# Hybrid attention and convolution step: 38 of 64 input-projection tiles computed in pairs by seven block products, conv taps spread into the attention

## The chip, the cores and the metric

One core of a Trainium2 chip runs the whole kernel. PE multiplies matrices (PEld is its loading of stationary operands), DVE and ACT work element by element, POOL too but cannot read PSUM, and SP issues nearly all DMAs. The metric is the device time of one execution in microseconds, as the median of several runs. Profiled executions come with a trace, from which all times by engine and line are read.

## The reference

The layer is one inference step of a streaming encoder, for 1024 new frames of one stream and 32 frames of a running one; the kernel puts them side by side as 1056 tokens. All data is float32.

```python
q = rmsnorm(cols(OFF_Q, ATTN_WIDTH).reshape(B, T, N_HEADS, HEAD_DIM), q_g) * (HEAD_DIM ** -0.5)
k = rmsnorm(cols(OFF_K, ATTN_WIDTH).reshape(B, T, N_HEADS, HEAD_DIM), k_g)
v = cols(OFF_V, ATTN_WIDTH).reshape(B, T, N_HEADS, HEAD_DIM)
logf = jax.nn.log_sigmoid((cols(OFF_F, N_HEADS) + b_f).astype(jnp.float32))
ga = cols(OFF_GA, ATTN_WIDTH)
u = cols(OFF_UA, CONV_WIDTH) * jax.nn.sigmoid(cols(OFF_UB, CONV_WIDTH))
gb, ma, mb = cols(OFF_GB, CONV_WIDTH), cols(OFF_MA, D_MODEL), cols(OFF_MB, D_MODEL)
...
ya = (o_attn.reshape(B, T, ATTN_WIDTH) * jax.nn.silu(ga)) @ w_pa
yb = (jax.nn.silu(layernorm(conv, ln_g, ln_b)) * jax.nn.silu(gb)) @ w_pb
m = jax.nn.sigmoid(ma) * ya + jax.nn.sigmoid(mb) * yb
return x + m @ w_out
```

`cols(a, w)` is `rmsnorm(x) @ w_in[:, a:a + w]`. `o_attn` is causal softmax attention of 16 heads of 64 with a bias from the running sum of `logf`; `conv` is a causal depthwise convolution of `u` over 31 taps. The widths are 1024, so eight of the nine projections are 1024 x 1024 (`logf` has 16 columns), and three more such products follow the branches.

## The kernel before

**Plain projections.** `xh` and `xl` hold the normalised input as a high part (float32r) and a remainder, with 8 blocks of 128 channels on the partitions and 1056 tokens in a row. A *tile* is 128 output channels of one projection: `steps` (L144) takes its weights, split by ACT into `wh` (L91) and by POOL into the remainder `wl` (L94), and multiplies over three pieces of 352 tokens and 8 channel blocks. Each of these 24 steps is three matmuls (`mms`, L102): xh by wh, xh by wl, xl by wh. A tile is so 72 matmuls of 352 columns. The nine projections but `v` and `logf` make 64 tiles: ub, ua, k, q, ga, gb, ma, mb, 8 each. `v` and `logf` are computed the other way round, with 260 weight columns moving (L582).

**Order.** PE, DVE and ACT follow program order up to the attention, and PE all through. `beat` (L118) is called once a step: it runs what `later(n, fn)` put off by n beats, and adds `pace["rate"]` to a credit from which *conv taps* are paid. A tap (`conv_taps`, L248) is one DVE instruction on 128 x 1086 elements (L258); 30 of them and one ACT instruction make the convolution of one channel tile f, and then come its LayerNorm sums (`sums`: L228, L235, L236, L241).

**Stages.** The input is normalised and turned while the first ub and ua tiles run (to 44 us). Then come u tiles 1 and 2 among the four parts of v (to 193 us), u tile 3, and for each f the k and q tiles, with u tiles 4 to 7 between them. `qk` (L678) squares each piece on ACT, sums squares by head with two small matmuls (L697, L698), takes the root on ACT (L700, L701), scales on DVE (L704) and stores high and low parts for the attention (L714, L715). Then u tile 7 and the 8 ga tiles (to about 591 us). In these stages taps of channel tiles 0 to 6 run on DVE beside the matmuls.

**Attention** (591 to 1095 us). Per head there are 8 blocks of 128 queries, and 4 blocks of the running stream among them. A block's scores (L905, L906) go to PSUM three blocks ahead of its use; DVE adds the mask and takes the maximum (L908, L910), ACT the exponentials (L913), DVE the reciprocal (L915), POOL the scaling (L916); PE turns the result (L926) and multiplies by V (L940). Between blocks PE does 4 steps of a plain tile (`fill`); 22 tiles (gb, ma, 6 of mb) are done so. The 31 taps of channel tile 7 and its sums run here, one tap for each 8 steps, and then the LayerNorm statistics (`layernorm`, one step a block).

**End.** Two mb tiles, then the three products of the branches (`outproj`), 8 tiles each.

Of the kernel before, what the change touches and what calls it, by code (L numbers as in the profile page):

```python
# [16 lines left out]
T = 1024  # L17
TS = 32
# [12 lines left out]
NFILL = 22  # L31
R_U, R_V, R_QK, R_G, R_A = 0.25, 0.17, 0.19, 0.27, 0.12
# [16 lines left out]
def build(tc, xT, xt, wv, wf, ckT, cv, clT, stT, vec, cst, yT, kT, vO, lfO, cpT, csT):  # L49
# [19 lines left out]
    s_m = dram.tile([128, TT], F32, name="s_m")  # L69

    cp = pool("cp")
    wp = pool("wp", 2)
# [3 lines left out]
    rawp = [wp]  # L76
# [11 lines left out]
    def split_w(raw, offset=2000):  # L88
        with tc.high_priority(offset=offset):
            wh = wp.tile([128, KT, 128], F32R, name="wh", tag="wh")  # L90
            nc.scalar.copy(wh, raw)  # L91
            wl = wp.tile([128, KT, 128], F32R, name="wl", tag="wl")
            for k0, k1 in WSP:
                nc.gpsimd.tensor_sub(wl[:, k0:k1, :], raw[:, k0:k1, :], f32(wh[:, k0:k1, :]))  # L94
        return wh, wl
# [40 lines left out]
    def fetch():  # L136

        if plan:
            key = plan.pop(0)
            if not plan:  # L140
                rawp[:] = [wp]
            split[key] = split_v(key[1]) if key[0] == "v" else split_w(load_raw(key))
# [27 lines left out]
    sg = pool("sg")  # L170

    def t352(name, bufs):
        return sg.tile([128, CH], F32, name=name, tag=name, bufs=bufs)

    pq = pool("pq", 1, space=PS)
    pps = ExitStack()
    pjA = pool("pjA", 4, stack=pps, space=PS)
# [15 lines left out]
    cvp = pool("cvp", 2, stack=pcv)  # L193
    us = {}
    taps = []
    cvt = [cvp]
# [9 lines left out]
    def shift_of(y):  # L206

        shift = cvp.tile([128, TT], F32, name="shift", bufs=1)
        ones = cvp.tile([128, 128], F32, name="ones", bufs=1)
# [8 lines left out]
        nc.sync.dma_start(s_m, shift)  # L218
# [28 lines left out]

    def conv_taps(f):  # L248
        u = us.pop(f)

        def tap(i):
            w = vec_t[:, V_WDW + f * KC + i:V_WDW + f * KC + i + 1]
            if i == 0:
                y = sides["y", f] = cvt[0].tile([128, CW], F32, name="y", tag="y")
# [3 lines left out]
            t = nc.vector.scalar_tensor_tensor(y, u[:, i:i + CW], w, y, op0=ALU.mult, op1=ALU.add)  # L258
            if f == 7:
                tc.keep_in_program_order(t)  # L260
            if i == KC - 1:
                kept(f, y)

        items = [lambda i=i: tap(i) for i in range(KC)]
        if f == 7:
            taps.extend(pend + items)
# [11 lines left out]
    def u_tile(f):  # L278
        if f > 2:
            pump(len(taps) - 66)  # L280
        u = us[f] = cvt[0].tile([128, UW], F32, name="u", tag="u", bufs=3 if f < 7 else 1)
# [4 lines left out]
    def u_done(f):  # L286
        u = us[f]
# [71 lines left out]
    os_t = cp.tile([128, 8, TS], F32, name="os_t")  # L359
# [116 lines left out]
    plan.extend([("ub", 1), ("ua", 1), ("v", 0), ("v", 1), ("ub", 2), ("ua", 2), ("v", 2), ("v", 3), ("ub", 3), ("ua", 3)])  # L476
    for f in range(8):
        if f in (2, 4, 6):
            plan.extend([("ub", 3 + f // 2), ("ua", 3 + f // 2)])
        plan.extend([("k", f), ("q", f)])  # L480
    plan.extend([("ub", 7), ("ua", 7)] + [("ga", f) for f in range(8)] + [("gb", 0)])
# [23 lines left out]
    prw = ExitStack()  # L505
    rxs = [pool(f"rx{i}", 1, stack=prw) for i in range(2)]
    rawp.extend(rxs)
# [3 lines left out]
    p2 = ExitStack()  # L511
    u7p = pool("u7p", 1, stack=p2, side="right")
    pv = ExitStack()
    zp = pool("zp", 1, stack=pv, side="right")
    z = zp.tile([128, 9, H], F32, name="z")
# [45 lines left out]
    for c in range(4):  # L561
        if c == 2:
            pace["rate"] = R_U
            u_proj(2, pj)
            while ("y", 0) not in sides or len(taps) > 62:
# [28 lines left out]
    fp = pool("fp", 1, stack=pv, side="right")  # L594
# [3 lines left out]
    def small(name):  # L598
        return fp.tile([128, NZ], F32, name=name, tag=name)

    lf = fp.tile([128, 9, H], F32, name="lf")
    lfs = lf, lf.rearrange("p a b -> p (a b)")

    def log_sigmoid():
        lf, lff = lfs
        az, ee, s2, ac = small("az"), small("ee"), small("s2"), small("ac")
# [19 lines left out]
        chores.extend([(0.3, op) for op in ops] + [(0.0, forget_sums)])  # L626

    def forget_sums():

        lfT = fp.tile([H, TT], F32, name="lfT")  # L630

        def turned(c):
            pt = tr.tile([128, 512], F32, name="ptr", tag="tr")
# [4 lines left out]
            chores.append((0.4, lambda: nc.vector.tensor_copy(lfT[:, c * 512:c * 512 + w], pt[:H, :w])))  # L638
# [3 lines left out]
        for c in range(3):  # L642
            later(14 * c + 8, lambda c=c: turned(c))

    def forget_rows(lfT):
        on16 = fp.tile([H, T], F32R, name="on16")
        nc.gpsimd.memset(f32(on16), 1.0)
        ls = fp.tile([H, SKEYS], F32, name="ls")
        nc.sync.dma_start(ls[:, :PAST], clT)
        cc = fp.tile([H, T], F32, name="cc")  # L650
        csm = fp.tile([H, SKEYS], F32, name="csm")
        ch, cl, nch, ncl = [fp.tile([H, T], F32R, name=n) for n in ("ch", "cl", "nch", "ncl")]
        V = nc.vector
        ops = [
            (1.4, lambda: V.tensor_tensor_scan(cc, f32(on16), lfT[:, :T], 0.0, op0=ALU.mult, op1=ALU.add)),
            (0.1, lambda: V.tensor_copy(ls[:, PAST:], lfT[:, T:])),
            (0.8, lambda: (V.tensor_tensor_scan(csm, f32(on16)[:, :SKEYS], ls, 0.0, op0=ALU.mult, op1=ALU.add),
                           nc.sync.dma_start(s_cs, csm))),
            (0.8, lambda: V.tensor_copy(ch, cc)),
            (0.8, lambda: V.tensor_sub(cl, cc, f32(ch))),  # L660
            (0.8, lambda: V.tensor_scalar(nch, f32(ch), -1.0, None, op0=ALU.mult)),
            (0.8, lambda: V.tensor_scalar(ncl, f32(cl), -1.0, None, op0=ALU.mult)),
        ]

        def out():
            for dst, rows in ((s_aq, (on16, on16, ch, cl)), (s_ak, (nch, ncl, on16, on16))):
                for i, rw in enumerate(rows):
                    nc.sync.dma_start(dst[:, i, :], f32(rw))
# [4 lines left out]
        chores.extend(ops + [(0.0, out)])  # L673


    pqk = ExitStack()
    tp = pool("tp", 2, stack=pqk, side="right")
    def qk(g, f):  # L678
        gv, dst, smp = (vec_t[:, V_KG:V_KG + 1], s_k, ks_t) if g == "k" else (qg8, s_q, qs_t)
        qn = tp.tile([128, TT], F32, name="qn", tag="qn")  # L680

        def ev(c, sl, ps):
            sqf = tp.tile([128, CH], F32, name="sqf", tag="sqf")
            sqh = tp.tile([128, CH], F32R, name="sqh", tag="sqh", bufs=3)
            sql = tp.tile([128, CH], F32R, name="sql", tag="sql", bufs=3)
            nc.scalar.activation(sqf, ps, AF.Square)
            nc.scalar.copy(sqh, sqf)

            def low():
                nc.vector.tensor_sub(sql, sqf, f32(sqh))  # L690

            later(2, low)
            later(11, lambda: root(c, sl, ps, sqh, sql))

        def root(c, sl, ps, sqh, sql):
            pm = st.tile([128, 512], F32, name="pst", tag="st")
            nc.tensor.matmul(pm[:, :CH], bones, sqh, start=True, stop=False)  # L697
            nc.tensor.matmul(pm[:, :CH], bones, sql, start=False, stop=True)  # L698
            ri = tp.tile([128, CH], F32, name="ri", tag="ri")
            nc.scalar.activation(ri, pm[:, :CH], AF.Ln, bias=eps_t, scale=1.0 / HD)  # L700
# [546 lines left out]
```

## Time and profile before

| | |
|---|---|
| median of 3 runs | 1405.24 us (1404.52 to 1405.7) |
| the profiled execution | 1405.11 us |
| its span, first to last instruction | 1403.3 us |
| mean granted clock of PE | 0.999 |
| PE busy | 1390.1 us, 99% |
| DVE, ACT, POOL busy | 866.0, 604.2, 617.5 us |
| HBM | 136 GB/s over the span |

Matmuls are pipelined: one starts before the one before it has ended, so the busy times of single matmuls add up to more than the time that passes. What a matmul costs in a dense row is read from the chain of work, which gives the time that a number of them took together. DVE and POOL rows hold the time from an instruction's start to its end, in which it may have waited for a memory port; an instruction's shortest time over the run is near what it takes with no one beside it.

### The profile page before, as it was taken

The numbers are of one execution on the slowest core, as the hardware profiler recorded it, in microseconds if no ns is written. First come the engines' busy times: TensorE is split into PE (matmuls) and PEld (weight loads), VectorE is DVE, ScalarE is ACT, GpSimd is POOL, SyncE is SP. The second block draws the span as 40 slices with busy tenths as digits, with TensorE's granted clock in tenths as the row PEclk, the third lists the DMA queues.
The fourth block names the chain that finished last, engine by engine and source line by source line (L and its number), as shares of the span: only waits on it lengthen the run. The fifth ranks groups of instructions, "written<-read, shape, count | busy, mean of one in ns | idle before, by whom it ended". The sixth has DMA issues, their size and how long they took to land.

```text
span 1403.3 us, 23422 instructions
## 1 busy us (share of the span) xinstructions
PE 1390.1 (99%) x8999; PEld 1303.6 (93%) x8999; DVE 866.0 (62%) x1199; ACT 604.2 (43%) x1180; POOL 617.5 (44%) x541
## 2 busy tenths in 40 slices
PE   8999999999999999999999999999999999999999
PEld 7999999999999999998888888878888999999998
DVE  6687787888898998646655656644444497132111
ACT  6322334646464642245454546544554455232100
POOL 2324254557585875343433433232332366254320
PEclk9999999999999999999999999999999999999999
DMA  4242333424342484335545546353532778444431
GB/s 181 92 141 92 119 108 99 160 76 142 106 152 92 138 194 150 111 100 129 148 107 160 146 136 177 101 154 109 155 115 73 276 254 271 143 138 142 150 108 47
DMA packets 102288, 192.77 MB, mean 137 GB/s; under 512 B 17248, under 2 KB 70368, under 8 KB 102176
## 3 DMA queue, kind: packets, MB, share of 16 engines
q1 hardware_dynamic: 102032, 191.21, 44.4%
q8 instruction: 71, 1.16, 0.4%
q14 instruction: 41, 0.34, 0.1%
q10 hardware_dynamic: 144, 0.07, 0.0%
HBM read 125.58 MB, written 65.64 MB: 136 GB/s over the span
## 4 chain that ended last, share of the span: by engine, by line
PE 92%; issue 3%; DVE 2%; ACT 2%; POOL 1%; DMA 1%; SPq 0%; ACTq 0%; POOLq 0%; DVEq 0%
PE pj L102 67%; PE pjv L582 7%; PE po L940 5%; PE ptr L926 4%; PE psS L905 3%; PE psS L906 2%; POOL wl L94 1%; PE pst L698 1%; PE pst L697 1%; PE po L885 0%; DVE y L1082 0%; PE ptx L427 0%; DMA xtok<-xt 0%; ACT xh L429 0%; PE pjs L541 0%
## 5 line engine op out<-in xcount | busy, mean ns | idle before, releaser
L102 PE MATMUL pj<-xh,wh 128*128 128x352 f32 (+2 forms) x1536 | 510.0, 332 | 1.7 <-ACT t L753 1.1
L102 PE MATMUL pj<-xh,wl 128*128 128x352 f32 (+2 forms) x1536 | 494.0, 322 | 1.9 <-POOL wl L94 1.9
L102 PE MATMUL pj<-xl,wh 128*128 128x352 f32 (+2 forms) x1536 | 495.5, 323 | 0.2
L94 POOL TENSOR_TENSOR wl<-raw,wh 128x384 fp32r<-128x384 f32 (+1 forms) x258 | 323.1, 1280 | 258.1 <-ACT wh L91 226.9
L258 DVE SCALAR_TENSOR_TENSOR y<-u,vec_t,y 128x1086 f32<-128x1086 f32 x240 | 382.5, 1594 | 23.7 <-ACT y L255 19.6
L102 PEld LDWEIGHTS pj<-xh,wh 128*128 128x128 f32 x1536 | 289.0, 188 | 10.2 <-ACT t L753 6.6
L102 PEld LDWEIGHTS pj<-xh,wl 128*128 128x128 f32 x1536 | 289.9, 189 | 2.5 <-POOL wl L94 2.2
L102 PEld LDWEIGHTS pj<-xl,wh 128*128 128x128 f32 x1536 | 289.1, 188 | 1.4 <-DVE xl L430 1.2
L916 POOL TENSOR_SCALAR P<-P,nm 128x128 f32<-128x128 f32 (+7 forms) x128 | 107.6, 842 | 283.3 <-DVE nm L915 216.9
L91 ACT CAST wh<-raw 128x1024 fp32r<-128x1024 f32 x86 | 90.1, 1048 | 111.2 <-PE pj L102 80.5
L913 ACT ACTIVATE P<-psS,nm 128x128 f32<-128x128 f32 (+7 forms) x128 | 95.4, 745 | 70.7 <-DVE nm L910 61.5
L910 DVE TENSOR_REDUCE nm<-psS 128x1 f32<-128x128 f32 (+7 forms) x128 | 96.8, 756 | 8.6
L908 DVE TENSOR_TENSOR psS<-psS,cmask 128x128 f32<-128x128 f32 x128 | 38.1, 297 | 100.3 <-PE psS L906 99.3
L929 ACT COPY pt<-ptr 128x512 f32<-128x512 f32 (+3 forms) x128 | 65.0, 508 | 75.8 <-PE ptr L926 75.1
L715 POOL TENSOR_TENSOR ql<-qn,qh 128x352 fp32r<-128x352 f32 (+1 forms) x48 | 66.0, 1374 | 68.0 <-ACT qh L714 54.9
L926 PE MATMUL ptr<-ident,P 128*128 128x128 f32 x576 | 84.2, 273 | 0.0
L940 PE MATMUL po<-pt,V 128*64 128x512 f32 (+1 forms) x384 | 75.8, 530 | 0.0
L926 PEld LDWEIGHTS ptr<-ident,P 128*128 128x128 f32 x576 | 69.1, 140 | 5.6 <-issue 0.4
L582 PE MATMUL pjv<-vwh,xh 128*128 128x260 f32 x256 | 72.5, 283 | 0.0
L582 PE MATMUL pjv<-vwl,xh 128*128 128x260 f32 x256 | 72.4, 283 | 0.0
L582 PE MATMUL pjv<-vwh,xl 128*128 128x260 f32 x256 | 72.3, 282 | 0.0
L905 PE MATMUL psS<-KB,QB 128*128 128x256 f32 (+2 forms) x192 | 70.1, 366 | 0.6 <-ACT t L751 0.6
(200 smaller groups left out, 2237.4 us busy)
## 6 DMA issues: line engine op xcount, KB each, us to landing
raw<-wf SPq DMA_DIRECT2D x88, 512.0 KB
QB<-s_q SPq DMA_DIRECT2D x32, 256.0 KB
KB<-s_k SPq DMA_DIRECT2D x32, 256.0 KB
kT<-qn SPq DMA_DIRECT2D x8, 528.0 KB
s_ga<-t SPq DMA_DIRECT2D x24, 176.0 KB
s_gb<-t SPq DMA_DIRECT2D x24, 176.0 KB
s_ma<-t SPq DMA_DIRECT2D x24, 176.0 KB
s_mb<-t SPq DMA_DIRECT2D x24, 176.0 KB
```

The source lines that it names most:

```text
L91: nc.scalar.copy(wh, raw)
L94: nc.gpsimd.tensor_sub(wl[:, k0:k1, :], raw[:, k0:k1, :], f32(wh[:, k0:k1, :]))
L102: nc.tensor.matmul(ps, a[:, kt, :], b(kt, sl), start=(first and n == 0), stop=(last and n == N - 1))
L258: t = nc.vector.scalar_tensor_tensor(y, u[:, i:i + CW], w, y, op0=ALU.mult, op1=ALU.add)
L582: nc.tensor.matmul(ps[:, :VC], a, b, start=(n == 0), stop=(n == 23))
L715: nc.gpsimd.tensor_sub(ql[:, :n], qn[:, o], f32(qh[:, :n]))
L905: nc.tensor.matmul(ps[:, b, :wm], QB[:, qsl], KB[:, ksl], start=True, stop=False)
L910: nc.vector.tensor_reduce(nm[:, 0:1], ps[:, :nb, :w], axis=AX.XY, op=ALU.max, negate=True)
L913: nc.scalar.activation(P[:, :nk].rearrange("p (b w) -> p b w", b=nb), ps[:, :nb, :w], AF.Exp, bias=nm[:, 0:1], accum_out=nm[:, 1:2])
L916: nc.gpsimd.tensor_scalar(P[:, :nk], P[:, :nk], nm[:, 2:3], 1.0, op0=ALU.mult, op1=ALU.mult)
L926: nc.tensor.transpose(pt[:, 128 * j:128 * j + 128], P[:, 128 * (4 * u + j):128 * (4 * u + j) + 128], ident)
L940: nc.tensor.matmul(po[64 * o:64 * o + 64, q0:], V[:, j + o, hd], p[:, j + o, q0:], start=(j == 0), stop=(j == njb - 2), skip_group_check=True)
```

## The change

A *pair* is two tiles (k and q of one f, ub and ua of one f, or two neighbours of ga or gb) with the same 1024 input channels. Its weights are seen as 2 x 2 blocks of 512 channels by 128 outputs (a11, a12, a21, a22), and x as 2 x 2 blocks of 512 channels by 528 tokens. Eight block products would give the pair; seven do, of sums and differences of blocks (Strassen's scheme in Winograd's form). Nineteen pairs are made so, between v and the attention: gb 0 and 1, then for each f k and q and one other pair, then two more of gb. Ahead of them stay u tiles 0 to 3 and v; 18 plain tiles are left (gb 6 and 7, ma, mb), of which 16 fill the attention and 2 come at its end.

**Weights** (`prepare`, `w_sum`, `w_split`): DVE makes four sums of 128 x 512 for a pair, ACT casts the seven operands, POOL makes their low parts, 22 beats ahead of use. **Input** (`t_build`): while u tiles 2 and 3 run, DVE, ACT and POOL build t2, t3 and t4, with high and low parts, for four channel blocks; t1 then takes the place of one block of `xh` and `xl`, which has been saved to DRAM and comes back 19 beats ahead of the attention.

**Products** (`products`): a product is 24 matmuls of 264 columns (2 pieces by 4 channel blocks by 3), three to a beat. Four accumulators of two PSUM banks each (A to D) take the seven; ACT and DVE combine them at set beats (`at`): `p1_out` and `c11` on ACT, `n2_out`, `v3_out`, `c22`, `c21`, `c12` on DVE. `Keys` norms k and q by halves of 528 tokens, reading the combined values from SBUF; `Inputs` makes u, `Gates` stores ga and gb.

**Taps**: the rate is 0.1 a step in the products, and 0.3 in the attention (before 0.12). u tiles 4 to 7 go to DRAM and come back when their taps are due. `fill` does 3 steps a block where it did 4, and stops at the end of a piece of 352 tokens. Other pools are placed anew; `shift` stays in SBUF.

```diff
-NFILL = 22
-R_U, R_V, R_QK, R_G, R_A = 0.25, 0.17, 0.19, 0.27, 0.12
+NFILL = 16
+R_U, R_V, R_T, R_S, R_A = 0.3, 0.25, 0.19, 0.1, 0.3
+HB = 264
+HT = 2 * HB
+SPILL = 4
...
+    def t_build(j):
+        b11, b12, b22 = [tm.tile([128, HT], F32, name=a, tag=a) for a in ("b11", "b12", "b22")]
+        t1 = t1f[:, j, :]
...
+        joined(b12, j, HI)
+        joined(b22, 4 + j, HI)
...
+        return [lambda: nc.vector.tensor_add(b11, f32(xh[:, j, LO]), f32(xl[:, j, LO])),
+                lambda: nc.vector.tensor_sub(t1, b11, b12),
+                lambda: (nc.vector.tensor_sub(b12, b12, b22), nc.scalar.copy(t3[0][:, j, :], b12)),
+                lambda: (nc.vector.tensor_add(b22, b22, t1), nc.scalar.copy(t2[0][:, j, :], b22)),
+                lows,
+                lambda: nc.vector.tensor_sub(t2[1][:, j, :], b22, f32(t2[0][:, j, :])),
+                lambda: (nc.vector.tensor_sub(b11, b11, b22), parts(t4, j, b11))]
...
+    others = [("ub", 4, "ua", 4), ("ub", 5, "ua", 5), ("ub", 6, "ua", 6), ("ub", 7, "ua", 7), ("ga", 0, "ga", 1),
+              ("ga", 2, "ga", 3), ("ga", 4, "ga", 5), ("ga", 6, "ga", 7)]
+    pairs = [("gb", 0, "gb", 1)]
+    for i in range(8):
+        pairs += [("k", i, "q", i), others[i]]
+    pairs += [("gb", 2, "gb", 3), ("gb", 4, "gb", 5)]
+    BP = 56
+    LEAD = 22
...
+    def w_split(i, k):
+        raw = W[i][PROD[k][0]]
+        with tc.high_priority(offset=2000):
+            wh = pw.tile([128, 4, 128], F32R, name="swh", tag="swh", bufs=4)
+            nc.scalar.copy(wh, raw)
+            wl = pw.tile([128, 4, 128], F32R, name="swl", tag="swl", bufs=4)
+            nc.gpsimd.tensor_sub(wl, raw, f32(wh))
+        W[i][k] = wh, wl
+
+    def prepare(i):
...
+        s = S0[0] + i * BP
+        at(s - 30, lambda: w_sum(i, "s1", "a21", "a22", "s1"))
+        at(s - 27, lambda: w_sum(i, "s2", "s1", "a11", "s2"))
+        at(s - 24, lambda: w_sum(i, "s3", "a11", "a21"))
+        at(s + 23, lambda: w_sum(i, "s4", "s2", "a12"))
+        for k in range(7):
+            at(s + 8 * k - LEAD, lambda k=k: w_split(i, k))
+
+    PROD = (("a11", "b11", 0, True, True), ("s2", "t2", 1, True, True), ("s3", "t3", 2, True, True),
+            ("s1", "t1", 3, True, True), ("a12", "b21", 0, False, True), ("a22", "t4", 2, False, True),
+            ("s4", "b22", 3, False, True))
...
+        for t, fn in ((9, p1_out), (18, n2_out), (26, v3_out), (34, lambda: p.block(1, 1, c22)),
+                      (42, lambda: p.c11(ps[0])), (50, lambda: p.block(1, 0, c21)), (58, lambda: p.block(0, 1, c12))):
+            at(s + t, fn)
+        for k, (wn, xn, b, first, last) in enumerate(PROD):
+            wh, wl = W[i].pop(k)
+            oh, ol = OPS[xn]
+            if first:
+                ps[b] = bank("ABCD"[b])[:, :, :HB]
+            for c in range(2):
+                for kt in range(4):
+                    for n, (a, x) in enumerate(((wh, oh), (wl, oh), (wh, ol))):
+                        nc.tensor.matmul(ps[b][:, c, :], a[:, kt, :], x(kt, c), start=(first and kt == 0 and n == 0),
+                                         stop=(kt == 3 and n == 2), skip_group_check=not first)
+                    beat()
...
+    e = s + NP * BP
+    at(e - 62, to_heads)
+    at(e - 19, restore)
+    for i in range(NP):
+        products(i)
...
-            next(flow, None)
+            if next(flow, None):
+                break
...
-            fill(4 if b.i > 2 or b.head.h != 8 else 0)
+            fill(3)
```

More of the change, by code (lines that the diff above doesn't have):

```diff
@@ L562, in build @@
         if c == 2:
-            pace["rate"] = R_U
-            u_proj(2, pj)
-            while ("y", 0) not in sides or len(taps) > 62:
+            while ("done", 0) not in sides:
                 pump(1)
```

518 lines of the change are left out of this document (346 added, 172 removed).

## The prediction

> **What bounds the kernel now.** I read the page's busy shares first, then who waited on PE, busy time by stretch, and the chain in order of time. The page:
>
> ```profile
> span 1403.3 us, 23422 instructions
> PE 1390.1 (99%) x8999; PEld 1303.6 (93%) x8999; DVE 866.0 (62%) x1199; ACT 604.2 (43%) x1180; POOL 617.5 (44%) x541
> PE 92%; issue 3%; DVE 2%; ACT 2%; POOL 1%; DMA 1%; SPq 0%; ACTq 0%; POOLq 0%; DVEq 0%
> ```
>
> PE has work all the time and holds 92% of the chain that ended last. The two longest entries of PE's waits (us in total, times, longest) are small:
>
> ```profile
> PE pj L102 <- POOL wl L94: 3.4, 4, 1.9
> PE ptx L427 <- DVE xl L430: 1.8, 2, 1.5
> ```
>
> Stretches (length, then busy us of PE, PEld, DVE, ACT, POOL, granted clock): the k, q and gate projections, a piece of them, and the attention.
>
> ```profile
> 225.00:573.00 348.00, 347.60 (x2180) 346.77 (x2180) 306.07 (x286) 177.20 (x323) 228.34 (x161) 1.00 0.43 132
> 493.00:507.00 14.00, 14.00 (x90) 14.00 (x89) 13.82 (x11) 6.02 (x11) 14.00 (x9) 1.00 0.40 133
> 591.00:1095.00 504.00, 501.59 (x3256) 427.08 (x3256) 268.13 (x589) 246.59 (x542) 179.01 (x206) 1.00 0.46 130
> ```
>
> So what shortens PE's queue shortens the kernel, as long as DVE (88% busy over 225 to 573) and POOL (66%) keep up. Two dense runs of matmuls in the chain give PE's price, since overlapping busy times don't:
>
> ```profile
> 86.51 32.62 PE pjv L582 x270
> 491.28 76.45 PE pj L102 x481
> ```
>
> 260 columns: 32.62/270 = 0.1208 us each. 352 columns: 76.45/481 = 0.1589. The slope is 0.000414 us a column, so 264 columns cost an estimated 0.1225.
>
> **The change, part by part.** *PE.* Around the head norms (L697, L698; after: L930, L931) on PE's queue, with the semaphores waited for; before:
>
> ```order
> L102 MATMUL pj<-xl,wh 128x352
> L697 MATMUL pst<-sqh,bones 128x352 [waits Activation_49]
> L698 MATMUL pst<-sql,bones 128x352 [waits DVE_49]
> L102 MATMUL pj<-xh,wh 128x352
> L102 MATMUL pj<-xh,wl 128x352 [waits Pool_49]
> ```
>
> The end of one product and the start of the next pair, now:
>
> ```order
> L930 MATMUL psB<-sb,bones 128x264 [waits PE_49,Activation_49]
> L931 MATMUL psB<-sa,bones 128x264 [waits DVE_49]
> L1000 MATMUL psD<-xl,swh 128x264
> L1000 MATMUL psA<-xh,swh 128x264 [waits PE_49,Activation_49]
> L1000 MATMUL psA<-xh,swl 128x264 [waits Pool_49]
> ```
>
> Each product waits for its own weight halves from ACT and POOL, and for the bank that DVE or ACT empties. The halves have four buffers, so ACT's cast for product k waits until PE is through product k - 4, two beats (0.7 us) ahead of it in the plan; bank copies and norms queue behind that cast. From there POOL has 22 beats, 8.1 us, for a subtraction of 1.3 to 2.1. A pair took 2 x 72 = 144 matmuls of 352 columns and takes 7 x 24 = 168 of 264. Over 19 pairs: 2736 x 0.1589 = 434.8 us out, 3192 x 0.1225 = 391.0 in. The norms go from 96 x 0.1589 = 15.3 to 128 x 0.1225 = 15.7. Net -43.4 us.
>
> The Trainium skill (TensorE: Matmul & The Clock Gate, "Back-to-back issue gap") gives sustained spacings of 81 ns at 128 columns and 131 at 512; on a line between them 264 columns would take 99 ns and 352 take 110, an estimate by which the change would cost 315 - 302 = 13 us of PE. The rows above disagree at both widths (121 and 159 ns), so they decide, and the rule gets no chance here.
>
> *DVE and POOL while the products run.* DVE's queue in a k and q stretch before (L258 taps, L690 low halves, L704 scaling from PSUM):
>
> ```order
> L258 SCALAR_TENSOR_TENSOR y<-u,vec_t,y 128x1086
> L690 TENSOR_TENSOR sql<-sqf,sqh 128x352
> L258 SCALAR_TENSOR_TENSOR y<-u,vec_t,y 128x1086
> L704 SCALAR_TENSOR_TENSOR qn<-pj,qg_193,ri 128x352
> L690 TENSOR_TENSOR sql<-sqf,sqh 128x352
> ```
>
> And between two pairs now (L751 weight sums, L975 to L984 the combining of products, L261 taps):
>
> ```order
> L975 TENSOR_TENSOR n<-psB,v 128x528
> L261 SCALAR_TENSOR_TENSOR y<-u,vec_t,y 128x1086
> L751 TENSOR_TENSOR rawa<-s_3435,rawa 128x512
> L924 TENSOR_TENSOR sa<-sf,sb 128x528
> L751 TENSOR_TENSOR s_3691<-rawb 128x512
> L978 TENSOR_TENSOR v<-psC,n 128x528
> L751 TENSOR_TENSOR s_3709<-s_3691,rawa 128x512
> L261 SCALAR_TENSOR_TENSOR y<-u,vec_t,y 128x1086
> ```
>
> Fewer taps, more adds, and bank B, C or D stays taken until L975, L978 or L984 gets its turn. Durations (min/median/max; by shape: busy, mean):
>
> ```profile
> L258 DVE SCALAR_TENSOR_TENSOR y<-u,vec_t,y x240: 1326/1351/3541, 52.9 to 820.8; 128x1086 f32<-128x1086 f32 x120
> L690 DVE TENSOR_TENSOR sql<-sqf,sqh x48: 488/561/1970, 220.8 to 489.3; 128x352 fp32r<-128x352 f32 x48
> L946 DVE TENSOR_TENSOR ot<-ot,po x32: 668/686/692, 632.4 to 1095.6; 64x512 f32<-64x512 f32 x32
> L235 DVE TENSOR_TENSOR mean<-mean,y 128x1024 f32<-128x1024 f32 x7 | 8.8, 1260 | 0.0
> L532 POOL TENSOR_TENSOR vwl<-vraw,vwh x16: 1295/2136/2368, 62.0 to 158.5; 128x520 fp32r<-128x520 f32 x16
> L94 POOL TENSOR_TENSOR wl<-raw,wh x258: 717/1017/2383, 34.9 to 1379.8; 128x384 fp32r<-128x384 f32 x86, 128x256 fp32r<-128x256 f32 x43
> L241 POOL TENSOR_TENSOR rstd<-rstd,y x14: 235/1848/2812, 201.8 to 831.5; 128x1024 f32<-128x1024 f32 x7, 128x32 f32<-128x32 f32 x7
> ```
>
> DVE alone: 96 taps x 1.33 = 128; 246 ops of 512 to 528 (75 weight sums, 32 low halves, 32 scalings, 12 for u, 95 reading PSUM) x 0.68 = 167; four tiles' LayerNorm sums 4 x (2 x 1.26 + 2 x 0.2) = 12; forget gates about 5. Together 312 of the stage's 391. POOL alone: 133 low halves and 32 of k and q x 1.30 = 215, sums and samples about 17: 232. Either fits, but an op with both inputs in SBUF is longer while the other engine runs one. Inside 225 to 573: taps and low halves on DVE (busy, count), POOL's low halves of the weights; then DVE beside POOL in the densest piece:
>
> ```profile
> 225.00:573.00 348.00, 214.62 (x131) 1.00 0.43 132
> 225.00:573.00 348.00, 38.77 (x47) 1.00 0.43 132
> L94 POOL TENSOR_TENSOR wl<-raw,wh 128x384 fp32r<-128x384 f32 x58 | 93.4, 1629 | 34.4 <-ACT wh L91 34.3
> L94 POOL TENSOR_TENSOR wl<-raw,wh 128x256 fp32r<-128x256 f32 x29 | 45.8, 1579 | 0.0
> 495.89 7.30 DVE L258 SCALAR_TENSOR_TENSOR y<-u,vec_t,y 128x1086 f32<-128x1086 f32 x4
> 494.26 5.83 POOL L94 TENSOR_TENSOR wl<-raw,wh 128x384 fp32r<-128x384 f32 x3
> ```
>
> A tap there costs 214.62/131 = 1.64, 0.31 over alone; a low half 0.82, 0.33 over; in the dense piece 7.30/4 = 1.83, 0.50 over. (L946 and the other readers of PSUM stay within 25 ns.) The stage has 263 such DVE ops: 312 + 263 x 0.31 = 394 us, or x 0.50 = 443. POOL's alone-time rises from 40% in the k and q stretch (a low half of n columns alone takes 0.72 + 0.00219 x (n - 256), by the shortest of L94 and L532: 58 x 1.00 + 29 x 0.72 + 48 x 0.91, 13 for sums and samples, 135 of 348) to 59%, which pushes up; the 95 PSUM readers in between let POOL run, which pushes down. I take 0.36, nearer the 348 us mean than a 12 us piece: 407, **+16** over PE's 391 (bounds +3 and +52).
>
> *ACT*, in the same stage: 133 casts of half the size (1.048/2), five ops for each of 32 norm halves, 17 table loads:
>
> ```profile
> L91 ACT CAST wh<-raw 128x1024 fp32r<-128x1024 f32 x86 | 90.1, 1048 | 111.2 <-PE pj L102 80.5 <-issue 20.2 <-POOL wl L94 7.6
> L700 ACT ACTIVATE ri<-pst,eps_t 128x352 f32<-128x352 f32 x48 | 26.6, 555 | 31.8 <-PE pst L698 31.8
> L727 ACT ACT_TABLE_LOAD x5 | 6.4, 1283 | 0.1
> ```
>
> 70 + 32 x 5 x 0.7 + 22 + about 45 of copies and gates = 249 of 391: hidden.
>
> *Building the operands* (under the u projections of channel tiles 2 and 3, 96 x 3 x 0.1589 = 45.8 us): 36 DVE ops of 528 (24.5), 17 small ones of the forget gate (17 x 0.4 = 7), multiplies and weight sums (7), taps (4): 43, and 45 of them at 0.31 make 57. DVE is some 11 us late at the first product; the last four splits (4) and PE's 2.9 us until t2 is read are free. Bounds 0 and 11: **+5**.
>
> ```profile
> L619 DVE SCALAR_TENSOR_TENSOR ac<-ac,s 128x144 f32<-128x144 f32 x7 | 3.3, 476 | 0.2
> DMA packets 102288, 192.77 MB, mean 137 GB/s; under 512 B 17248, under 2 KB 70368, under 8 KB 102176
> ```
>
> *Transfers.* To DRAM and back go t1's place in x (4 x 1.08 MB) and four u tiles (8 x 0.57): 9 MB beside 192.77, on a queue with the DMA engines 0.43 busy in 225 to 573. SP sends them in order; a u tile is needed only when its taps come up, tens of us later. Nothing, but for one place:
>
> *Start of the attention.* The part of x that t1 overwrote (2 x 1.08 MB) is issued 19 beats, 7 us, ahead; PE reads it 4.3 us into the attention. At the 275 GB/s below it takes 8 us, at 130 it takes 17 (bounds 0 and 6): **+2**.
>
> ```profile
> 1095.00:1203.00 108.00, 106.43 (x650) 105.02 (x651) 72.70 (x63) 60.29 (x73) 58.49 (x34) 1.00 0.81 275
> L908 DVE TENSOR_TENSOR psS<-psS,cmask 128x128 f32<-128x128 f32 x128 | 38.1, 297 | 100.3 <-PE psS L906 99.3
> ```
>
> *Attention.* 6 plain tiles fewer take 69 us from its 504 (already in the -43.4). Taps rise from 30 to 81: DVE goes from 268 to about 268 + 51 x 1.4 + 7 = 346 of 435 us. L908's row shows DVE waiting on PE for 99 us; that idle time hides the taps, at 0.1 us for some 30 of 132 blocks: **+3** (bounds 0 and 20).
>
> Sum: 1403.3 - 43.4 + 16 + 5 + 2 + 3 = 1385.9 us of span; the profiled execution took 1405.11, 1.8 outside its span, against a median of 1405.24. That makes **1387.7, say 1388**.
>
> **Rivals.** *PE stays the bound:* DVE waits no more than in 225 to 573 and every extra stays under 4: 1361.7 + 0 to 15. For it: PE lost nothing in the 14 us when DVE and POOL were both full. Against: 59% of POOL.
>
> *The products run at DVE's pace, and it gets slower.* Each SBUF op is served behind POOL's, as in the dense piece, for the whole stage: 443, +52, and with the other +10 1361.7 + 62 = 1424. It decides from 424 us, where a wait is 0.43: then the net gain of 43.4 is gone. For it: both queues would be nearly full for 390 us. Against: 0.31 over 348 us. If the two shut each other out whole, DVE's 241 us of SBUF ops and POOL's 232 make 473, and 1454; a tap and a wl piece at once took 1.94 (5.83/3) against 1.33 + 1.00 apart, so not whole (0.03 of this rival's 0.18). The Trainium skill (SBUF — State Buffer, "Who interferes with whom") calls it an exclusive lock on a shared port pair; by that rule the 473 holds, and the trace goes only most of the way.
>
> *Given back in the attention:* taps stand ahead of mask, max or reciprocal, and each of 132 blocks loses another 0.12: +16, 1404. For it: block time falls from 3.82 to 3.30 us. Against: DVE still idles 20%.
>
> **How the numbers follow.** Forecast (1377 to 1399) 0.45; PE bound (1362 to 1377) 0.25; given back (1398 to 1410) 0.12; slower at DVE's pace (over 1408) 0.18. The range starts at no losses, 1362, and ends at 0.45 a wait (430, +39) with +10, 1411. A change of 0.2% is 2.8 us, about what a measurement here can tell. Faster 0.45 + 0.25 + 0.06, same 0.07, slower 0.17.
>
> **What would show it.** Right: 0.122 us a matmul at 264 columns, a products stage of 400 to 415 us with DVE over 97% busy, and PE waiting on L975 to L987. PE over 99% busy there means the first rival; taps at 1.83 and a stage over 424 the second. Wrong altogether: matmuls of 264 columns at over 0.135 us (they then eat the saving), or PE waiting on POOL's low halves or DMA instead.

## The result and the profile after

The changed kernel takes **1453.82 us** (median of 4 runs, 1452.64 to 1457.06) beside 1404.88 of the kernel before (4 runs, 1402.71 to 1405.7): a ratio of 1.0354, with a 95% interval of 1.0334 to 1.0375. It is slower by 49 us, where 1388 and a gain of 17 were forecast, and lies outside the range of 1362 to 1411. The page of its profiled execution (1452.64 us), span, busy shares and the chain of work that ended last:

```profile
span 1450.8 us, 24814 instructions
PE 1367.0 (94%) x9487; PEld 1268.6 (87%) x9487; DVE 1046.3 (72%) x1368; ACT 648.5 (45%) x1209; POOL 749.4 (52%) x557
PE 45%; DVE 16%; ACT 5%; issue 5%; DMA 5%; POOL 3%; SPq 0%; DVEq 0%; ACTq 0%; POOLq 0%
```

PE's share of the chain fell from 92% to 45%, with DVE next (the shares listed add up to 79% of the span): the matmuls alone no longer set the end. Two stages lost the time. Busy times from the first to the last product, and from the first scores to the last product by V (columns as in the prediction, behind the clock the DMA share and GB/s):

```profile
222.50:682.00 459.50, 423.87 (x3331) 415.63 (x3332) 413.40 (x375) 238.04 (x377) 323.20 (x200) 0.98 0.37 124
681.80:1127.60 445.80, 417.26 (x2692) 340.09 (x2690) 338.32 (x649) 229.29 (x513) 208.88 (x179) 0.98 0.49 138
```

And the attention of the kernel before, by the same two marks:

```profile
605.00:1095.00 490.00, 488.42 (x3185) 414.20 (x3185) 268.13 (x589) 245.12 (x539) 173.98 (x196) 1.00 0.46 128
```

The products' 3320 matmuls (norms included) need 3320 x 0.1225 = 407 us and took 459.5. The attention has 495 plain matmuls fewer than before (1090 of them, against 1585, between the marks), so it should have taken 490.0 - 495 x 0.1589 = 411 us, and took 445.8. Lost are 52 and 35 us. With the 5.6 us ahead of the first product (below) that is 93 us, about the 91 by which the span of 1450.8 lies above 1403.3 - 43.4. Whom PE waited for in the whole run (us in total, times, longest us):

```profile
PE psS L1198 <- ACT P L1206: 22.8, 10, 5.6
PE psB L930 <- DVE n L975: 7.3, 4, 2.5
PE psC L1000 <- POOL swl L759: 5.9, 1, 5.9
PE psA L1000 <- DVE u L314: 5.6, 1, 5.6
PE psD L1000 <- DVE t L981: 3.7, 5, 1.7
```

The first row is the attention, where scores wait for a bank that the exponential has not read. The fourth is the first product, behind the operand building. The rest is the products stage: DVE is late with a combination, or POOL with the low part of a weight. DVE in turn, and ACT, in that stage:

```profile
DVE sa L924 <- DMA s_q<-sa: 10.0, 6, 2.2
DVE sa L924 <- ACT sb L921: 7.9, 9, 1.4
DVE rawa L751 <- POOL swl L759: 6.5, 2, 3.6
```

```profile
ACT sb L946 <- DVE qn L943: 51.6, 16, 6.8
ACT swh L757 <- DVE rawa L751: 39.1, 9, 5.5
```

DVE is busy for 413 of 459.5 us. In the other 46 it waits for others, longest for a store and a cast, while ACT waits for DVE for 91 us in its two longest rows alone. Its taps in the two stages, then in the first of them the weight sums, POOL's low parts, and n2 (L975, which reads PSUM), each as length of the stage, busy time and count:

```profile
222.50:682.00 459.50, 177.78 (x99) 0.98 0.37 124
681.80:1127.60 445.80, 117.97 (x81) 0.98 0.49 138
222.50:682.00 459.50, 82.29 (x73) 0.98 0.37 124
222.50:682.00 459.50, 228.78 (x131) 0.98 0.37 124
222.50:682.00 459.50, 13.27 (x19) 0.98 0.37 124
```

A tap takes 1.80 us beside the products (1.33 alone, the shortest), a sum 1.13, a low part 1.75 (1.30 alone). An n2 takes 0.70, as an operation of that size does alone.

### The profile page after: what moved, and what is told of

Same layout as the page of the kernel before. It is cut to its first block, busy times and chain, and to the rows that moved or that the text cites. A ratio compares the mean times of both kernels' runs of the same rounds, so it can differ in the third digit from the quotient of the medians.

```text
span 1450.8 us, 24814 instructions
## 1 busy us (share of the span) xinstructions
PE 1367.0 (94%) x9487; PEld 1268.6 (87%) x9487; DVE 1046.3 (72%) x1368; ACT 648.5 (45%) x1209; POOL 749.4 (52%) x557
## 4 chain that ended last, share of the span: by engine, by line
PE 45%; DVE 16%; ACT 5%; issue 5%; DMA 5%; POOL 3%; SPq 0%; DVEq 0%; ACTq 0%; POOLq 0%
PE pj L107 25%; DVE y L261 5%; PE po L1233 4%; PE psA L1000 3%; PE ptr L1219 3%; PE psS L1198 2%; PE psS L1199 2%; PE psD L1000 2%; DVE s L751 1%; PE psC L1000 1%; PE psB L1000 1%; DVE nm L1203 1%; DVE y L1367 1%; POOL wl L99 1%; DMA s_y<-y 1%
## 5 line engine op out<-in xcount | busy, mean ns | idle before, releaser
L99 POOL TENSOR_TENSOR wl<-raw,wh 128x384 fp32r<-128x384 f32 x141 | 160.2, 1164 | 197.0 <-ACT wh L96 181.4
L107 PE MATMUL pj<-xh,wh 128*128 128x352 f32 (+3 forms) x624 | 216.7, 347 | 4.6 <-ACT wh L96 2.2
L107 PE MATMUL pj<-xh,wl 128*128 128x352 f32 (+3 forms) x624 | 203.0, 325 | 1.0 <-POOL wl L99 1.0
L107 PE MATMUL pj<-xl,wh 128*128 128x352 f32 (+3 forms) x624 | 203.5, 326 | 0.2 <-DVE xl L439 0.2
L107 PEld LDWEIGHTS pj<-xh,wh 128*128 128x128 f32 x624 | 118.6, 190 | 10.3 <-ACT t L1100 3.5
L107 PEld LDWEIGHTS pj<-xh,wl 128*128 128x128 f32 x624 | 119.0, 191 | 2.2 <-POOL wl L99 1.8
L107 PEld LDWEIGHTS pj<-xl,wh 128*128 128x128 f32 x624 | 118.5, 190 | 1.8 <-DVE xl L439 1.8
L759 POOL TENSOR_TENSOR swl<-rawa,swh 128x512 fp32r<-128x512 f32 x57 | 93.1, 1635 | 48.2 <-ACT swh L757 37.7
L1000 PE MATMUL psA<-xh,swh 128*128 128x264 f32 x304 | 88.2, 290 | 9.7 <-DVE u L314 5.6
L1000 PE MATMUL psD<-xh,swh 128*128 128x264 f32 x304 | 88.5, 291 | 6.8 <-DVE t L981 3.7
L1198 PE MATMUL psS<-KB,QB 128*128 128x256 f32 (+2 forms) x192 | 72.2, 377 | 22.8 <-ACT P L1206 22.8
```

Of the source, the lines that this page charges most:

```text
L107: nc.tensor.matmul(ps, a[:, kt, :], b(kt, sl), start=(first and n == 0), stop=(last and n == N - 1))
L759: nc.gpsimd.tensor_sub(wl, raw, f32(wh))
L1000: nc.tensor.matmul(ps[b][:, c, :], a[:, kt, :], x(kt, c), start=(first and kt == 0 and n == 0), stop=(kt == 3 and n == 2), skip_group_chec ...
L1198: nc.tensor.matmul(ps[:, b, :wm], QB[:, qsl], KB[:, ksl], start=True, stop=False)
```

## The experiments

The theory T1: the products stage is set by DVE's queue, whose operations with two inputs in SBUF are stretched by POOL's and stretch POOL's. Its rivals: R1, the chain of a weight block (ACT's cast, POOL's low part) is late by itself; R2, DVE has too much to do, contention or not. For the attention, A1: taps and sums delay the blocks; A2: three fill steps a block are too few. And C: stalls of PE cost half-clock time on top. The kernel before took 1402.5 to 1403.0 us in each of these series.

**Without the taps of the products stage.**

```
+            if "attention" in sides or "products" not in sides:
                 t = nc.vector.scalar_tensor_tensor(y, u[:, i:i + CW], w, y, ...)
```

> The changed kernel without the 99 conv taps that VectorE issues in the products stage (178 us of its time there); they are left out of the computation, everything else stays. Theory T1 (the products stage is set by VectorE's queue, whose operations that read two SBUF inputs are stretched by GpSimd's and stretch GpSimd's): the stage falls from 459 us to 395 to 410 us, close to the 391 us of its matmuls, and the whole to 1385 to 1400 us; GpSimd's 512-element subtraction falls from 1.75 us towards 1.4 us. Rival R1 (the chain of a weight block, ScalarE's copy then GpSimd's subtraction, is late whatever VectorE does): the stage stays above 440 us and the whole above 1430 us, with TensorE waiting for the low parts. Rival R2 (VectorE has too much work, contention or not): as T1 here, but GpSimd's subtraction keeps its 1.75 us.

1403.39 us, ratio 1.0006 (0.9997 to 1.0016). The stage, then POOL's low parts in it:

```profile
222.60:633.30 410.70, 408.33 (x3331) 406.79 (x3332) 225.84 (x277) 244.27 (x377) 266.75 (x200) 0.99 0.41 139
222.60:633.30 410.70, 199.36 (x131) 0.99 0.41 139
```

The stage is within 4 us of PE's 407, and a low part falls from 1.75 to 1.52 us, though nothing was done to POOL: against R1, and against R2 in so far as taps slow POOL. Stage and whole lie 0.7 and 3 us above the ranges that T1 gave.

**Without POOL's low parts.**

```
-            wl = pw.tile([128, 4, 128], F32R, name="swl", ...)
-            nc.gpsimd.tensor_sub(wl, raw, f32(wh))
-        W[i][k] = wh, wl
+        W[i][k] = wh, wh
```

> The changed kernel without GpSimd's 133 subtractions that form the low parts of the weight blocks (229 us of GpSimd's time in the products stage); the high part stands in the place of the low one in the matmuls, so that TensorE has the same work and that part of the product is wrong. VectorE's instructions are the same in number and kind. Theory T1 (contention): the taps of the products stage fall from 1.80 us to 1.33 to 1.42 us, the stage from 459 us to 393 to 415 us, the whole to 1385 to 1410 us. Rival R2 (VectorE's volume alone): VectorE's work is unchanged, so the stage stays at 440 us or more and the whole above 1430 us. Rival R1 (the weight chain): the stage falls as in T1, but the taps stay at 1.7 us or more.

1401.95 us, ratio 0.9995 (0.9985 to 1.0005). The stage, its taps, its weight sums:

```profile
221.40:628.80 407.40, 406.37 (x3330) 405.81 (x3331) 318.38 (x375) 242.14 (x377) 87.18 (x67) 1.00 0.41 140
221.40:628.80 407.40, 136.81 (x99) 1.00 0.41 140
221.40:628.80 407.40, 51.15 (x73) 1.00 0.41 140
```

DVE issues the same 375 operations and needs 318 us for them instead of 413: a tap 1.38, a sum 0.70. The volume alone fits into the stage, so R2 falls. The row also prices the matmul: 407.4/3330 = 0.1223 us.

**The low parts made, but waited for by no matmul.** The last run takes away the contention and the chain at once; this one takes only the chain.

```
             nc.gpsimd.tensor_sub(wl, raw, f32(wh))
-        W[i][k] = wh, wl
+        W[i][k] = wh, wh
```

> The changed kernel in which GpSimd still makes the low parts of the weight blocks, but no matmul waits for them or reads them: the high part stands in their place, so that part of the product is wrong. VectorE's and GpSimd's work are as in the changed kernel, TensorE's too; only the chain from weight block over GpSimd to TensorE is cut. Theory T1 (VectorE and GpSimd stretch each other, and VectorE's queue sets the pace): the products stage stays at 445 to 462 us and the whole at 1438 to 1456 us, taps at 1.75 us or more. Rival R1 (the late chain of a weight block set the pace): the stage falls to 407 to 420 us as it did without the subtractions, and the whole under 1415 us.

1444.59 us, ratio 1.0294 (1.0268 to 1.0321):

```profile
222.00:677.20 455.20, 422.48 (x3330) 414.11 (x3331) 413.56 (x375) 237.89 (x377) 324.43 (x200) 0.98 0.38 127
```

DVE and POOL are as busy as in the changed kernel, a tap takes 1.81 us, and the stage is as long but for 4 us: R1 falls, T1 stands.

**Half of the stage's taps moved into the attention.** In this kernel the taps end so late that the last sixth of the LayerNorm's root is left out.

```
-R_U, R_V, R_T, R_S, R_A = 0.3, 0.25, 0.19, 0.1, 0.3
+R_U, R_V, R_T, R_S, R_A = 0.3, 0.25, 0.19, 0.05, 0.45
```

> The changed kernel complete, with the rate of taps halved in the products stage (0.05 for 0.1) and raised in the attention (0.45 for 0.3): about 50 taps move on from one to the other. Theory T1: the products stage loses about 50 x 1.8 = 90 us of VectorE's time and falls to 400 to 420 us; the attention, where VectorE already had 346 us of 445 us, takes 50 x 1.33 to 1.46 = 67 to 73 us more and grows by 15 to 45 us, so the whole is 1420 to 1450 us. Rival (the attention has the room that VectorE's idle time there shows): the attention stays within 5 us of 445 us and the whole is 1395 to 1412 us. Rival R1 (weight chain): the products stage stays above 440 us and the whole rises over 1455 us.

1423.7 us, ratio 1.0148 (1.0133 to 1.0163), stage and attention:

```profile
223.50:635.70 412.20, 409.68 (x3331) 408.45 (x3332) 318.82 (x318) 236.76 (x373) 274.38 (x196) 0.99 0.39 133
635.50:1100.40 464.90, 426.13 (x2692) 341.25 (x2690) 405.54 (x702) 233.84 (x515) 246.74 (x183) 0.97 0.49 138
```

As T1 expected: the stage gains 47 us, the attention loses 19 of them again.

**Without the taps of the attention, and then without its sums too.** The second has both edits; `go` calls its function only ahead of the attention.

```
-            t = nc.vector.scalar_tensor_tensor(y, u[:, i:i + CW], w, y, ...)
+            if "attention" not in sides:
+                t = nc.vector.scalar_tensor_tensor(y, u[:, i:i + CW], w, y, ...)
...
-        return [lambda: from_shift(f, sides["y", f]), lambda: into_sums(f, sides["y", f])]
+        return [lambda: go(from_shift), lambda: go(into_sums)]
```

> The changed kernel without the 81 conv taps that VectorE issues in the attention (left out of the computation; the LayerNorm sums of those channel tiles stay). The attention now takes 445.8 us; the kernel before took 490.0 with 495 more plain matmuls of 0.1589 us in it, so the same pace would give 411.3. Theory A1 (the taps and sums that stand ahead of mask, maximum and reciprocal on VectorE delay the blocks): the attention falls to 415 to 426 us, the whole to 1420 to 1435 us, and TensorE's waits for the exponentials shrink from 22.8 us to under 10. Rival A2 (three fill steps a block instead of four leave too little time for a block's chain, whatever VectorE does): the attention stays above 437 us and the whole above 1443 us. The products stage stays at 459 us in both.

> As the one before, and the LayerNorm sums that fall into the attention are left out too. Theory A1: the attention reaches 411 to 417 us, the whole 1412 to 1426 us, and there is at most one stall of TensorE over 2 us in the attention. Rival A2: still above 437 us. If the taps alone were the cause and the sums none, this is within 2 us of the run before.

1426.0 us, ratio 1.0164 (1.0149 to 1.0179), and 1422.87 us, ratio 1.0135 (1.0118 to 1.0152). The attention of the first, then of the second, then POOL's scaling of a block (busy, mean ns) in the first and in the changed kernel:

```profile
683.40:1101.20 417.80, 409.97 (x2692) 337.41 (x2690) 238.27 (x566) 228.30 (x513) 146.10 (x179) 0.99 0.52 145
```

```profile
684.70:1097.70 413.00, 408.11 (x2691) 336.74 (x2690) 227.14 (x556) 224.81 (x509) 135.85 (x173) 1.00 0.52 145
```

```profile
L1208 POOL TENSOR_SCALAR P<-P,nm 128x128 f32<-128x128 f32 (+7 forms) x128 | 96.7, 759 | 227.1 <-DVE nm L1207 196.6
```

```profile
L1209 POOL TENSOR_SCALAR P<-P,nm 128x128 f32<-128x128 f32 (+7 forms) x128 | 144.5, 1134 | 195.8 <-DVE nm L1208 182.0
```

A1 holds: of 35 us the taps make 28 and the sums 5, and three fill steps a block are enough. PE's waits for the exponentials fell from 22.8 to 4.9 us in the first. Taps also make POOL's scaling, a step in each block's chain, 0.38 us longer; how much of the 28 us comes that way, and how much by DVE's order, no run separates.

**The sums in two places**, 8 and 11 taps into the next tile.

```
...
-            taps.extend(items[:4] + pend + items[4:])
+            taps.extend(items[:8] + pend[:1] + items[8:11] + pend[1:] + items[11:])
```

> The changed kernel complete, with the LayerNorm sums of a channel tile moved from one place, 4 taps into the next tile, to two places, 8 and 11 taps into it (their store to DRAM is then done, and VectorE does not do them in one block). If the stalls in the attention come from this clump (the longest, 5.6 us, has both subtractions and both sums of one tile and a wait for its store ahead of a mask): attention 430 to 440 us, the whole 1435 to 1449 us. If they come from the taps as such: attention 443 to 448 us and the whole within 3 us of 1453.8. The products stage stays within 5 us of 459 in both.

1446.78 us, ratio 1.031 (1.0295 to 1.0326). The whole lies in the range of the first expectation, but for another reason: the products stage fell to 455.1 us, and the attention, at 444.8, is where the second put it. DVE beside PE's longest wait there, now 6.3 us:

```profile
763.77 2.61 DVE L227 TENSOR_TENSOR y<-y,shift 128x1024 f32<-128x1024 f32 x2 [1.50 <-DMA s_y<-y]
766.31 0.29 DVE L1201 TENSOR_TENSOR psS<-psS,cmask 128x128 f32<-128x128 f32 x1
```

In the attention only the taps are bound to program order on DVE; the sums came where they had come before, ahead of a mask and with the same wait for their store. Whether a real spread would help stays open.

**Twenty taps moved, and the sums as above.**

```
-R_U, R_V, R_T, R_S, R_A = 0.3, 0.25, 0.19, 0.1, 0.3
+R_U, R_V, R_T, R_S, R_A = 0.3, 0.25, 0.19, 0.075, 0.38
```

> The changed kernel complete, with the sums spread as in the run with that edit, and about 20 of 99 taps moved from the products stage into the attention (rates 0.075 and 0.38). By the runs so far a tap costs 0.5 us in the products stage while that is short of VectorE (48.8 us for 99), more for the first ones taken away than for the last, and 0.35 us in the attention (28 us for 81). Theory T1 with a products stage set by VectorE's queue: the first 20 taps give back their whole 1.8 us, so the stage falls to 418 to 432 us, the attention is 447 to 458 us, and the whole 1410 to 1430 us. Rival (a tap costs the same wherever it is, 0.3 to 0.5 us): the stage falls by 10 us at most and the whole is 1438 to 1450 us.

1421.44 us, ratio 1.0127 (1.0112 to 1.0142): products 425.9 us, attention 448.4, in the ranges of T1. The stage:

```profile
222.20:648.10 425.90, 414.17 (x3331) 408.84 (x3332) 372.66 (x347) 236.56 (x375) 301.25 (x198) 0.99 0.39 131
```

Not so its price of a tap. Beside the last run, which has the same sums, 25 taps fewer (75 against 100) make the stage 29 us shorter: 1.2 us a tap, and not the whole 1.8. The 49 taps moved above gave 47 us, the 99 left out no more than 49: what a tap gives falls as the stage nears PE's 407. DVE is busy for 88% of the stage here, as over 225 to 573 in the kernel before, where PE lost nothing; here PE still loses 19 us, so the share alone does not give the loss. It is the fastest complete version of the change here, and slower than the kernel before.

**The weight sums by accumulating DMAs.** Two versions, both complete: the four sums of a pair are loads onto which POOL issues DMAs that add; the second issues them earlier.

```
+        nc.gpsimd.dma_start(w[y], w[x], accum_op=ALU.add)
...
-        at(s - 30, lambda: w_sum(i, "s1", "a21", "a22", "s1"))
...
+        at(s - 38, lambda: w_add(i, "s1", "a22"))
```

> The changed kernel complete, with the four weight sums of a pair made by accumulating DMAs, issued by GpSimd, in place of VectorE's 76 additions (two more plain loads a pair; the last cast of a pair 4 beats later). VectorE loses 75 x 1.14 us = 86 us of its busy time in the products stage, 50 us of it work alone. Theory T1: the stage falls to 407 to 425 us and the whole to 1400 to 1420 us. Rival P (GpSimd pays for the DMAs what VectorE saves, 1 us or more for each of 76, and makes the low parts late): the stage stays above 440 us or rises, with TensorE waiting for the low parts. Rival R1: as P, since nothing in the chain of a weight block gets shorter.

> The changed kernel complete, with the weight sums by accumulating DMAs as before, but so that no cast waits for them: the first pair's sums stay on VectorE, the DMAs are issued 40, 28 and 4 beats ahead of the pair (a landing took 3.2 to 7.1 us, a beat is 0.37), the fourth sum goes into the place of a11 instead of a12, and the LayerNorm sums are spread as in the run with that edit. VectorE is rid of 72 additions (50 us alone, about 82 us beside GpSimd). If T1 holds and GpSimd bears 72 issues of 0.9 us: the products stage 410 to 430 us, the whole 1392 to 1418 us. Rival P (GpSimd, now at 303 us of work alone plus its waits, is late with low parts and issues, and its in-order queue holds up the casts as it did): the stage over 440 us and the whole over 1430 us.

1507.38 us, ratio 1.0736 (1.0717 to 1.0755), and 1468.19 us, ratio 1.0473 (1.0447 to 1.0499). What ACT waited for in the first, and PE behind it:

```profile
ACT swh L769 <- DMA s<-s: 88.2, 15, 10.3
ACT swh L769 <- DMA rawa<-s: 78.2, 18, 9.1
```

```profile
PE psB L943 <- ACT sf L952: 26.3, 6, 7.5
```

In the second the stage, one kind of issue, and where POOL sat idle before its issues:

```profile
222.00:700.10 478.10, 428.05 (x3331) 420.52 (x3332) 377.72 (x305) 237.66 (x377) 330.27 (x271) 0.96 0.68 188
```

```profile
L762 POOL DMA_DIRECT2D s<-s x18: 865/876/1207, 240.6 to 673.1; - x18
...
  DMA s<-wf: 43.2, 14
  DMA rawa<-wf: 26.4, 13
```

DVE is relieved (378 of 478 us), but POOL pays 0.88 us an issue and stands in its queue for loads; ACT waits for the landings and for POOL, and PE for ACT and DVE. The stages, 514.9 and 478.1 us, are those of rival P: the work went from one queue into others. P's sign is not there: PE waited for POOL's low parts for only 6.5 us in the first and 5.1 in the second.

**Stalls put into the kernel before.** Where DVE has room, 16 stalls of PE: the norm matmuls of the middle third of a k or q tile are issued 1 beat after it instead of 11, and for k ACT squares it three times.

```
-            later(11, lambda: root(c, sl, ps, sqh, sql))
+            later(1 if c == 1 else 11, lambda: root(c, sl, ps, sqh, sql))
```

> The kernel before, with 16 stalls put into its key and query tiles where VectorE has room: the two head-norm matmuls of the middle third wait at once for their operand instead of 11 k-tiles later; for the eight key tiles ScalarE squares that third three times over, so that these eight stalls are longer (about 3 to 4 us) than those of the query tiles (about 2 us). Theory C (a stall of 2.5 us or more is followed by 3.4 us at half the granted clock): each of the eight long stalls costs its own length and then 1.5 to 3 us more, in which a 352-column matmul takes 0.30 us or more instead of 0.159 us; the whole rises by 45 to 75 us. Rival (the half clock in the changed kernel has another cause, the length of the stage or the power drawn): matmuls behind the stalls keep 0.159 us and the whole rises by the stalls alone, 25 to 45 us.

1446.98 us in one run, 44 more than before: by the time alone in the rival's range, just below that of C. But the stalls were shorter than planned, 1.58 us for each of the eight k tiles, so the granted clock decides (1.00 is full speed). PE's waits, then PE's busy time (count), granted clock, DMA share and GB/s in four stretches around one such stall, and in two at another:

```profile
PE pst L698 <- ACT sqh L688: 21.4, 16, 4.6
PE pst L699 <- DVE sql L691: 5.0, 8, 1.3
```

```profile
220.00:223.40 3.40, 3.40 (x24) 1.00 0.49 154
223.40:226.70 3.30, 1.59 (x8) 1.00 0.00 0
226.70:230.10 3.40, 3.40 (x14) 0.50 0.02 5
230.10:233.50 3.40, 3.40 (x23) 1.00 0.00 0
```

```profile
390.50:393.90 3.40, 2.01 (x11) 1.00 0.43 152
393.90:397.30 3.40, 3.40 (x23) 1.00 0.00 0
```

The first stall left PE busy for half of one stretch of 3.4 us, and in the next stretch it ran at clock 0.50, 14 matmuls instead of 23. So a stall can bring half clock, as C has it, and one of 1.58 us is enough, not 2.5; but not each does, as the second shows. In size it is the small part: seven such stretches, one of 6.8 us, cost some 8 x 1.4 = 11 us, the waits 26; some 7 of the 44 us stay unexplained.

**No taps and sums in either stage**: the edits of the first experiment and of the two on the attention together.

```
+            if "products" not in sides:
                 t = nc.vector.scalar_tensor_tensor(y, u[:, i:i + CW], w, y, ...)
```

> The changed kernel without any conv tap in the products stage and in the attention, and without the LayerNorm sums that fall into the attention (all left out of the computation). By the sum of the two separate runs: products 407 to 412 us, attention 411 to 416 us, the whole 1366 to 1374 us, so that 80 us of the changed kernel's 1453.8 come from these taps and sums, and what stays over the 1362 us of TensorE's arithmetic is the 9 us at the first product. If there is a third loss that only shows when these two are gone, the whole stays above 1380 us.

1373.11 us, ratio 0.9784 (0.9768 to 0.98), products and attention:

```profile
222.70:635.00 412.30, 408.45 (x3331) 406.50 (x3332) 228.14 (x277) 244.75 (x378) 265.33 (x200) 1.00 0.42 143
634.80:1046.90 412.10, 408.25 (x2692) 336.71 (x2690) 227.20 (x556) 224.87 (x509) 136.12 (x173) 1.00 0.52 144
```

The two losses add up (50 and 31 us singly, 81 together), and no third one is hidden: the rest over 1362 is the first product's wait, 5.7 us here, and the 5 us by which these products, which start at half clock behind that wait, exceed 407.

## Why the prediction was wrong

*PE, -43.4 us:* right. A matmul of 264 columns in a dense stage costs 0.122 us, and with these taps and sums gone from DVE the kernel is 30 us faster than before, not 43, of which the next steps explain most.

*Products, +16 us: this step failed.* It made the stage as long as DVE's busy time, as if DVE were never idle, and let PE lose only the difference. DVE's work alone was right (312 forecast, 318 busy without POOL's low parts), and so in sum were its waits: 407 busy us forecast, 413 measured. A single wait, taken at 0.36 "nearer the 348 us mean than a 12 us piece", was 0.47 for a tap and 0.43 for a sum, near the dense piece, but the busy time came out only 6 us over. The stage was 46 us longer than that. For these 46 us DVE stood idle, in an order fixed ahead, behind a store, a cast or a low part, while ACT waited for DVE. Without POOL's low parts, or without the taps, stage and PE's 407 agree within 4 us. So the runs show that the loss needs both, taps and low parts, and that it is not PE's wait for the low parts; they do not show what each of DVE's idle waits costs.

The comparison was also crooked: PE's 391 left out the stage's norm matmuls (15.7 us, counted elsewhere in the sum), so that a DVE pace of 407 would have cost nothing at all. On paper two queues of 407 us stood beside each other, with no margin. Measured against PE's 407 the loss is 52 us; that this is also the term's upper bound (443 - 391) is chance. Right was that PE would wait for the combining operations; "DVE over 97% busy" was wrong (90%). PE also waited for POOL's low parts (5.9 us in one row above, 2.3 in another), the sign named for "wrong altogether"; with no matmul waiting for them the stage still took 455.

*Nearest to what happened* is the second rival, DVE's pace with longer waits. Its signs came: a stage over 424 us, and taps near 1.83 (1.80). It got 0.18. Its sum did not come: it takes DVE as busy for 443 us and never idle, and DVE was busy for 413 and idle for 46, which makes the stage 16 us longer than its price. The Trainium skill (SBUF — State Buffer, "Who interferes with whom") has the engines exclude each other whole on the shared ports, hence 473 us for this stage. By that rule operations that read PSUM are spared, and the trace agrees (0.70 us for n2); as a whole the stage stayed 14 us below 473, and that 1454 came out for the kernel is chance, since 35 us of it arose in the attention.

*Operands, +5 us (0 to 11):* right, 5.6 us and half clock after it. *ACT hidden:* right by its 238 busy us (249 forecast), but its queue passed DVE's delays on. *Start of the attention, +2 us:* no wait of PE for that transfer is in its list.

*Attention, +3 us (bounds 0 to 20): this failed too.* DVE's forecast load was right (346, measured 338), and its idle time was to hide the taps. What counts in a block, as the longest wait below shows, is not the idle share but what stands ahead of mask and maximum at the moment; there are 10 such waits of PE for the exponentials, 22.8 us together. That the taps and sums cost the 35 us is shown by leaving them out (413 us). The longest wait has a tap and the subtractions and sums of a whole channel tile ahead of a mask (PE's wait; some of what DVE did in it; busy times and clock from then on):

```profile
775.30 0.80 PE L1198 MATMUL psS<-KB,QB 128*128 128x512 f32 x1 [5.63 <-ACT P L1206]
```

```profile
767.58 2.15 DVE L227 TENSOR_TENSOR y<-y,shift 128x1024 f32<-128x1024 f32 x2 [1.30 <-DMA s_y<-y]
770.45 1.33 DVE L261 SCALAR_TENSOR_TENSOR y<-u,vec_t,y 128x1086 f32<-128x1086 f32 x1
772.34 1.31 DVE L234 TENSOR_TENSOR mean<-mean,y 128x1024 f32<-128x1024 f32 x2
773.57 0.29 DVE L1201 TENSOR_TENSOR psS<-psS,cmask 128x128 f32<-128x128 f32 x1
```

```profile
772.70:779.50 6.80, 4.20 (x15) 3.53 (x17) 6.13 (x12) 3.59 (x8) 4.63 (x4) 0.50 0.03 11
```

The rival "given back in the attention" had this mechanism at half its price (16 us) and as an alternative to the other; both came together.

## What to carry to other kernels

A scheme that saves matmuls is paid in element-wise work, so it is priced on the engine that does that work. Here a pair saves 43.4/19 = 2.3 us of PE and costs DVE nine operations of 0.68, 6 us alone, and more beside POOL; DVE was 88% busy in that stretch before. When two queues that wait for each other come out equally long on paper, the longer one is a lower bound and not the forecast: here 407 and 407 took 459.5, with DVE busy for 413. An engine's idle share does not say that work put there is free: ask what will stand behind it at the moment when it runs.

## What the runs showed of the hardware

*Half clock after short stalls.* The half-clock stretches in the stalled kernel before start at 226.7, 257.4 and 339.3 us, 9 and 33 times 3.41 apart: a fixed raster. The Trainium skill (TensorE: Matmul & The Clock Gate, "What's actually happening") has a free-running window of 3413 ns and the slow state after an idle window; the raster agrees, but here a window half busy was followed by half clock too. What counts, by these rows, is how much of one cell a stall empties: of the eight equal stalls of 1.58 us five were followed by half clock. In the first of them PE was busy for 1.59 of 3.30 us; in the one that was not and is shown above, which runs across the edge of a cell, it was busy for 2.01 of 3.40 us. The changed kernel's mean clock of 0.985 over 1450.8 us stands for some 43 us at half clock, a loss of at most half of it, 22 us of the 87.

*Contention both ways.* Without DVE's taps POOL's low part is 0.22 us shorter, without POOL's low parts DVE's tap is 0.41 us shorter, and POOL's scaling with a single SBUF tensor as input is stretched by taps too (0.76 to 1.13 us).
